# One change to a diffusion backbone kernel on one core: the entry of the first feed forward

## The chip, the core and the metric

The kernel runs on one core of a Trainium2 chip. The core has five engines with their own instruction queues: TensorE (PE, matrix products; PEld is its loading of weights), VectorE (DVE), ScalarE (ACT), GpSimd (POOL) and SyncE (SP, which here only issues transfers), and 16 DMA engines. The metric is device microseconds of one launch. Before the change: 2480.34 us, median of three runs (2479.79 to 2483.69).

## What is computed

Two layers over 640 tokens of width 1024 (512 latent tokens and 128 context tokens), in float32. Each layer is a half-step feed forward, a mixer (pooling, convolution and attention side by side), and a second half-step feed forward. Every one of the three is entered by a normalization and a modulation that depends on a condition vector. Cut to what matters here:

```
def _rms(x, g):
    y = xf * lax.rsqrt(jnp.mean(xf * xf, axis=-1, keepdims=True) + EPS)
    return (y * g.astype(jnp.float32)).astype(x.dtype)

def _modulations(cond, w, b):
    m = jax.nn.silu(cond) @ w + b
    return jnp.split(m[:, None, :], N_MOD, axis=-1)

    sh1, sc1, g1, sh2, sc2, g2, sh3, sc3, g3 = _modulations(cond, p['mod_w'], p['mod_b'])
    h = _rms(x, p['norm_g'][0]) * (1.0 + sc1) + sh1
    x = x + 0.5 * g1 * _swiglu(h, p['ffn1_wi'], p['ffn1_wo'])
    h = _rms(x, p['norm_g'][1]) * (1.0 + sc2) + sh2
    ...
```

For the first feed forward the shift sh1 and the scale sc1 (2048 columns of mod_w of layer 0, 8 MB) are needed before its first matrix product can start, and so is the mean of squares of each token.

## The kernel before

X lies transposed: partitions are features, in 8 chunks (k) of 128, and the free dimension is tokens, cut in two halves of 320. x arrives as five tiles of 128 tokens by 1024 (xt, L199 to L208), is transposed by PE into PSUM and copied to X by DVE.

Matrix products are in fp32 split in a high and a low part (wh, wl for weights; F_h, F_l for the input), three products for one. The feed forward's input has seven forms per pair of chunks (kp = 0 to 3, called quarters here), kept in four tiles F_h and four tiles F_l per layer step; later weight blocks use all seven, the first two blocks (f0 and f1, "plain", L596) only the plain ones.

The entry of the first feed forward (L1204 to L1235) goes like this. The squares of all eight chunks of X are taken by ACT and added by POOL (sq_chunk, L399), PE sums over partitions with a product with ones (r_ss), DVE computes the reciprocal root by three Newton steps (rsqrt), builds a diagonal matrix of it, and PE spreads it over all partitions (r_b), once for each half (rstd_half, L438). ACT copies it to R (L1211). Then, for each of four quarters t, two blocks of modulation weights are loaded (mw, 1 MB each: v = 1 is the scale, v = 0 the shift), PE multiplies them with the condition (mod, L282), DVE transposes the result, adds the bias (modv) and forms the scale a (scale_of). With these, first() and second() make the two halves' plain forms: DVE multiplies X by R (hf_x, hf_q), ACT applies scale and shift (affine, L465; POOL some pieces, L463), ACT and DVE split (F_h L457, F_l L458; hf_A21h and hf_A21l for the second half's even chunk). PE runs that quarter of block f0's four products (plain_step), and sums() makes the other four forms (hf_g). After the fourth quarter come the products of block f1, then the ordinary blocks from 2 on (L555).

Raw weights go through two buffers (tag raw, 8 KB per partition). Quarters 0 and 2 of the modulation weights take these buffers, quarters 1 and 3 take the buffers of F_h and F_l that are not written yet. Transfers are issued by SP in its program order. A scheduler with a timeline of its own decides the order of instructions on every engine from the order of the code and from priorities; so a change at the start can also move instructions far behind it.

Of the kernel before, what the change touches and what calls it, by code (L numbers as in the profile page):

```python
# [98 lines left out]
def backbone(ctx: ExitStack, tc: tile.TileContext, ins, consts, y_prompt, y_sample, out_k, out_v):  # L99
# [96 lines left out]
        par.update(qkg=qkg, sink=sink, nsink=nsink)  # L196


    for i in range(5):  # L199
        xt = act([P, D], F32, f"xt{i}")  # L200
        src = ins["x_sample"][0, i * P:(i + 1) * P, :] if i < 4 else ins["x_prompt"][0]
        nc.sync.dma_start(out=xt, in_=src)
        for q in range(2):
# [65 lines left out]

        return [lambda t=t: step(t) for t in range(4)]  # L270

    def modulation_block(ps, l, v, t, aside):

        if aside:
            raw = scope["pool"].tile([P, KD, 256], F32, tag=f"F{'hl'[v]}", name=f"mw_{l}_{v}_{t}", bufs=4)
        else:
            raw = wpool.tile([P, KD, 256], F32, tag="raw", name=f"mw_{l}_{v}_{t}", bufs=BUFS["raw"])
        nc.sync.dma_start(out=raw, in_=ins["mod_w"][l, :, v * D + 256 * t:v * D + 256 * (t + 1)].rearrange("(k p) f -> p k f", p=P))
        for k in range(KD):
            w = raw[:, k, :].rearrange("p (j g c) -> p j g c", g=4, c=32)  # L280
            for g in range(4):
# [34 lines left out]
            y = y2  # L316
        return y

    def rstd_diag(acc, n, name):

        ps = bank(name + "_ss")
        for i in range(5):
            PE.matmul(ps[:, i:i + 1], acc[:, i * P:(i + 1) * P], ones[:, 0:1], start=True, stop=True)
        v = small(name + "_v", 5)
        V.tensor_scalar(out=v, in0=ps[:, 0:5], scalar1=1.0 / n, scalar2=EPS, op0=ALU.mult, op1=ALU.add)
        y = rsqrt(v, 5, name)
        dg = tmp(name + "_dg")
# [108 lines left out]
    def rstd_half(acc, more, h, name):  # L438

# [774 lines left out]
    pm = [bank(f"mod_0_{v}", "ox"[v]) for v in range(2)]
    chains = [(0, c, h, "asat"[2 * c + h]) for c in range(2) for h in range(2)]
    for t in range(4):
        for v in (1, 0):
            modulation_block(pm[v], 0, v, t, t % 2 == 1)
        scale_of(0, 0, inp.a, slice(2 * t, 2 * t + 2))
        inp.first(R[:, 0:HALF], t)  # L1220
        inp.second(R[:, HALF:T], t)
# [97 lines left out]
```

## Time and profile before

| | |
|---|---|
| median of three runs | 2480.34 us |
| the profiled execution | 2478.26 us, of which 2476.5 us from first to last instruction |
| PE busy / PEld / DVE / ACT / POOL | 2348.3 / 2222.1 / 1707.3 / 1021.5 / 475.7 us |
| the chain that ended last, by engine | PE 82%, DVE 10%, ACT 4%, DMA 2% |
| mean granted clock of TensorE | 0.967 of 2.4 GHz |

Busy time of an engine says where it is full, not whether that matters. PE is the engine of nearly all of the chain, so time is lost where PE waits: in the first 85 us, in the two mixers (about 538 to 831 and 1746 to 2043 us) and a little at the start of the other feed forwards. Idle time of the other engines costs nothing by itself.

### The profile page before, as it was taken

To read this page: it belongs to the slowest core of one execution; us is meant where nothing else is said; L and a number is where in the kernel's file an instruction comes from. 1 tells how busy PE (TensorE), PEld (TensorE's weight loads), DVE (VectorE), ACT (ScalarE), POOL (GpSimd) and SP (SyncE) were. 2 spreads that over 40 slices of the span, in tenths; PEclk is the share of its full clock that TensorE was granted. 3 is DMA by queue.
4 is the path that set the end of the run, shared out by engine and by line. 5 is a ranking of instruction groups with operands and counts; after the bars stand their busy time and mean duration, and the time that the engine had idled before them with its cause. 6 is when DMAs were issued, how large, how long until landed. Compare 5 with 4: busy or idle time off the path is not lost.

```text
span 2476.5 us, 40450 instructions
## 1 busy us (share of the span) xinstructions
PE 2348.3 (95%) x16491; PEld 2222.1 (90%) x16491; DVE 1707.3 (69%) x3174; ACT 1021.5 (41%) x1865; POOL 475.7 (19%) x376
## 2 busy tenths in 40 slices
PE   4999999999888899999989999999988889999999
PEld 4899999998568899999989999999975789999998
DVE  4667676667875876676669484858588569585855
ACT  2433333344674533333345242425266545242423
POOL 2101020121431211111132020212024323020210
PEclk7999999999998999999999999999998899999999
DMA  5444332222512123342312424223243022222222
GB/s 172 131 141 132 98 125 69 92 94 91 181 63 71 49 94 128 104 133 94 121 61 82 141 82 141 86 86 101 73 148 134 22 77 69 86 82 81 86 77 77
DMA packets 193990, 246.04 MB, mean 99 GB/s; under 512 B 5705, under 2 KB 176494, under 8 KB 193804
## 3 DMA queue, kind: packets, MB, share of 16 engines
q1 hardware_dynamic: 191824, 240.81, 29.9%
q8 instruction: 130, 2.13, 0.4%
q0 software_dynamic: 512, 1.95, 0.3%
q10 hardware_dynamic: 1468, 0.70, 0.1%
q14 instruction: 56, 0.46, 0.1%
HBM read 240.55 MB, written 2.88 MB: 98 GB/s over the span
## 4 chain that ended last, share of the span: by engine, by line
PE 82%; DVE 10%; ACT 4%; DMA 2%; issue 2%; SPq 0%; POOL 0%; ACTq 0%; DVEq 0%; POOLq 0%
PE f_B L555 11%; PE o_a L379 11%; PE f_C L555 11%; PE o_b L379 11%; PE f_A L555 11%; PE f_D L555 6%; PE f L596 3%; PE p L743 2%; PE mod L266 2%; PE o L743 1%; PE u_q_b L379 1%; PE u_q_a L379 1%; DVE cy L930 1%; DVE xa_l L397 1%; DVE X L421 1%
## 5 line engine op out<-in xcount | busy, mean ns | idle before, releaser
L379 PE MATMUL o_a<-f_h,o_wh 128*128 128x320 f32 x1344 | 402.9, 310 | 0.0
L379 PE MATMUL o_b<-f_h,o_wh 128*128 128x320 f32 x1344 | 401.4, 309 | 0.0
L421 DVE SCALAR_TENSOR_TENSOR X<-o_a,gate,X 128x320 f32<-128x320 f32 x120 | 65.8, 549 | 305.3 <-PE o_a L379 305.0
L379 PEld LDWEIGHTS o_a<-f_h,o_wh 128*128 128x128 f32 x1344 | 251.0, 188 | 8.7 <-ACT o_wh L358 5.8
L547 POOL TENSOR_TENSOR f_t<-f 128x512 f32<-128x512 f32 x80 | 127.6, 1595 | 660.1 <-DMA f<-in_ffn_wi_dram 556.0
L379 PEld LDWEIGHTS o_b<-f_h,o_wh 128*128 128x128 f32 x1344 | 251.4, 188 | 2.9 <-issue 2.9
L358 ACT ACTIVATE o_wh<-wo 128x768 fp32r<-128x768 f32 (+1 forms) x120 | 95.9, 800 | 381.0 <-PE o_b L379 259.7
L654 POOL TENSOR_TENSOR f_t<-f_t,f 128x512 f32<-128x512 f32 x80 | 114.4, 1430 | 638.1 <-DVE f_q_wl L533 332.8
L379 PE MATMUL o_b<-f_h,o_wl 128*128 128x320 f32 x672 | 207.3, 308 | 0.0
L379 PE MATMUL o_a<-f_h,o_wl 128*128 128x320 f32 x672 | 207.0, 308 | 0.0
L531 ACT ACTIVATE f_q_wh<-f_t 128x512 fp32r<-128x512 f32 x140 | 85.9, 629 | 199.5 <-DVE f_t L545 55.0
L379 PEld LDWEIGHTS o_b<-f_h,o_wl 128*128 128x128 f32 x672 | 126.2, 188 | 0.0
L379 PEld LDWEIGHTS o_a<-f_h,o_wl 128*128 128x128 f32 x672 | 126.0, 188 | 0.0
L359 DVE TENSOR_TENSOR o_wl<-wo,o_wh 128x768 fp32r<-128x768 f32 (+1 forms) x120 | 108.2, 903 | 15.6 <-ACT o_wh L358 15.0
L934 POOL TENSOR_TENSOR cy<-cy,cm 128x655 f32<-128x655 f32 x52 | 88.7, 1705 | 148.4 <-ACT cm L933 148.4
L531 ACT ACTIVATE f_P_wh<-f 128x512 fp32r<-128x512 f32 x112 | 66.5, 626 | 120.2 <-PE f_A L555 78.2
L555 PE MATMUL f_B<-F_h,f_q_wl 128*128 128x320 f32 x352 | 108.7, 309 | 0.8 <-DVE f_q_wl L533 0.8
L555 PE MATMUL f_B<-F_h,f_q_wh 128*128 128x320 f32 x352 | 108.7, 309 | 0.2 <-ACT f_q_wh L531 0.2
L555 PE MATMUL f_B<-F_l,f_q_wh 128*128 128x320 f32 x352 | 108.6, 308 | 0.0
L555 PE MATMUL f_C<-F_h,f_m_wh 128*128 128x320 f32 x336 | 103.6, 308 | 0.0
L555 PE MATMUL f_C<-F_l,f_m_wh 128*128 128x320 f32 x336 | 103.6, 308 | 0.0
L555 PE MATMUL f_C<-F_h,f_m_wl 128*128 128x320 f32 x336 | 103.5, 308 | 0.0
(541 smaller groups left out, 7349.9 us busy)
## 6 DMA issues: line engine op xcount, KB each, us to landing
f<-in_ffn_wi_dram SPq DMA_DIRECT2D x88, 1024.0 KB, 5.2
mw<-in_mod_w_dram SPq DMA_DIRECT2D x72, 1024.0 KB, 5.1
wo<-in_ffn_wo_dram SPq DMA_DIRECT2D x48, 768.0 KB, 4.9
wo<-in_ffn_wo_dram SPq DMA_DIRECT2D x16, 512.0 KB, 3.4
wout<-in_w_out_dram SPq DMA_DIRECT2D x32, 256.0 KB, 3.2
win_q<-in_w_in_dram SPq DMA_DIRECT2D x4, 1024.0 KB, 5.1
xt<-in_x_sample_dram SPq DMA_DIRECT2D x4, 512.0 KB, 5.5
win_cg<-in_w_in_dram SPq DMA_DIRECT2D x2, 1024.0 KB, 5.1
```

The lines of the kernel that those rows point to most:

```text
L266: PE.matmul(ps[32 * g:32 * g + 32, 0:256], C[:, k, :], w[:, :, g, :], start=(k == 0), stop=(k == KD - 1))
L358: A.activation(out=wh, in_=src, func=AF.Copy)
L359: V.tensor_tensor(out=wl, in0=src, in1=wh.bitcast(F32), op=ALU.subtract)
L379: PE.matmul(ps[:, :n], ww[:, k, :], xx[:, lo:lo + n], start=(k == order[0] and i == 0), stop=(k == order[-1] and i == 2))
L421: V.scalar_tensor_tensor(out=X[:, m, s:e], in0=ps[:, s - o:e - o], scalar=gate[:, m, c:c + 1], in1=X[:, m, s:e], op0=ALU.mult, op1=ALU.add)
L531: A.activation(out=h, in_=src, func=AF.Copy, scale=sign)
L547: G.tensor_tensor(out=t3, in0=self.block(g, 1, 1), in1=self.block(g, 0, 1), op=ALU.add)
L555: PE.matmul(ps[:, :HALF], w[:, kp, :], self.F[f][kp][:, i, :], start=(first and kp == 0 and n == 0), stop=(kp == 3 and n == 2), skip_group ...
L596: PE.matmul(ps[:, :HALF], w[:, k, :], x, start=(k == 0 and n == 0), stop=(k == KD - 1 and n == 2))
L654: G.tensor_tensor(out=t2, in0=t2, in1=self.block(g, 1, 0), op=ALU.add)
L743: PE.matmul(ps[:, :HALF], w[:, m % 2, k, :], x[:, h * HALF:(h + 1) * HALF], start=(k == 0 and n == 0), stop=(k == 3 and n == 2))
L934: G.tensor_tensor(out=y, in0=y, in1=m, op=ALU.add)
```

## The change

Four things are done otherwise, all in the entry of the first feed forward.

1. The mean of squares: ACT squares each token tile xt as it arrives (1024 features along the free dimension) and sums along it, which gives one number per token with tokens on partitions. The eight squarings of X, POOL's additions and PE's sums over partitions go. The root is taken once for all five token tiles, and R is spread by rstd_spread, as in the mixers.
2. All eight modulation blocks of shift and scale are loaded at once, each into the buffer of F_h or F_l that the same quarter's form will use later (Input.open opens it after the block has been read).
3. The loads of blocks f0 and f1 are issued between them: f0 behind quarter 0, f1 behind quarter 2.
4. In the code a quarter's modulation products now stand ahead of the previous quarter's products.

```
+    ss00 = small("ss00", 5)
     for i in range(5):
         xt = act([P, D], F32, f"xt{i}")
...
         nc.sync.dma_start(out=xt, in_=src)
+        sq = wpool.tile([P, D], F32, tag="wl", name=f"sqx{i}", bufs=BUFS["w"])
+        A.activation(out=sq, in_=xt, func=AF.Square, accum_out=ss00[:, i:i + 1])
...
-    def modulation_block(ps, l, v, t, aside):
-
-        if aside:
-            raw = scope["pool"].tile([P, KD, 256], F32, tag=f"F{'hl'[v]}", name=f"mw_{l}_{v}_{t}", bufs=4)
-        else:
-            raw = wpool.tile([P, KD, 256], F32, tag="raw", name=f"mw_{l}_{v}_{t}", bufs=BUFS["raw"])
-        nc.sync.dma_start(out=raw, in_=ins["mod_w"][l, :, v * D + 256 * t:v * D + 256 * (t + 1)].rearrange("(k p) f -> p k f", p=P))
+    def modulation_block(ps, l, v, t, raw):
+
...
-    def rstd_diag(acc, n, name):
-
-        ps = bank(name + "_ss")
-        for i in range(5):
-            PE.matmul(ps[:, i:i + 1], acc[:, i * P:(i + 1) * P], ones[:, 0:1], start=True, stop=True)
+    def rstd_diag(acc, n, name, ss=None):
+
+        if ss is None:
+            ss = bank(name + "_ss")
+            for i in range(5):
+                PE.matmul(ss[:, i:i + 1], acc[:, i * P:(i + 1) * P], ones[:, 0:1], start=True, stop=True)
...
+        def __init__(self, l, j, kps=range(4)):
+            self.F, self.nm = ([], []), f"hf{l}{j}"
+            for kp in kps:
+                self.open(kp)
...
+        def open(self, kp):
+            for F, t in zip(self.F, "hl"):
+                F.append(new_form(f"F{self.nm}_{t}{kp}", t).rearrange("p (i t) -> p i t", i=7))
...
     phase("ffn00")
-    acc = tmp("acc00")
-    for k in range(KD):
-        sq_chunk(acc, k, f"sq00_{k}")
-    pbs = [rstd_half(acc, None, h, f"r00{h}") for h in range(2)]
-    R = work.tile([P, T], F32, tag="R", name="R00", bufs=1)
-    for h in range(2):
-        A.activation(out=R[:, h * HALF:(h + 1) * HALF], in_=pbs[h][:, :HALF], func=AF.Copy)
-    inp = Input(0, 0)
+    pm = [bank(f"mod_0_{v}", "ox"[v]) for v in range(2)]
+    inp = Input(0, 0, ())
     f = Ffn(0, 0, inp, ins["ffn1_wi"][0])
-    pm = [bank(f"mod_0_{v}", "ox"[v]) for v in range(2)]
-    chains = [(0, c, h, "asat"[2 * c + h]) for c in range(2) for h in range(2)]
+    raws = {}
     for t in range(4):
         for v in (1, 0):
-            modulation_block(pm[v], 0, v, t, t % 2 == 1)
+
+            raws[t, v] = new_form(f"mw_0_{v}_{t}", "hl"[v], F32)[:, 0:KD * 256].rearrange("p (k f) -> p k f", k=KD)
+            nc.sync.dma_start(out=raws[t, v], in_=ins["mod_w"][0, :, v * D + 256 * t:v * D + 256 * (t + 1)].rearrange("(k p) f -> p k f", p=P))
+        if t % 2 == 0:
+            f.load(t // 2)
+    R = rstd_spread(rstd_diag(None, float(D), "r00", ss00), work.tile([P, T], F32, tag="R", name="R00", bufs=1), [bank(f"r00_{t}", t) for t in "as"])
+    chains = [(0, c, h, "asat"[2 * c + h]) for c in range(2) for h in range(2)]
+
+    def modulations(t):
+        for v in (1, 0):
+            modulation_block(pm[v], 0, v, t, raws[t, v])
+
+    modulations(0)
+    for t in range(4):
+        inp.open(t)
         scale_of(0, 0, inp.a, slice(2 * t, 2 * t + 2))
         inp.first(R[:, 0:HALF], t)
         inp.second(R[:, HALF:T], t)
+        if t < 3:
+            modulations(t + 1)
```

What it does to the order of instructions shows at three places. The first is SP's queue behind x. In mw_0_1_2 the numbers are layer, v and quarter; f00_0 is block f0. Before:

```order
L278 DMA mw_0_1_0_267<-in_mod_w_dram 128x8x256
L278 DMA mw_0_0_0_304<-in_mod_w_dram 128x8x256
L346 DMA f00_0_364<-in_ffn1_wi_dram 128x8x256
L278 DMA mw_0_1_2_535<-in_mod_w_dram 128x8x256
L278 DMA mw_0_0_2_572<-in_mod_w_dram 128x8x256
L278 DMA mw_0_0_1_446<-in_mod_w_dram 128x8x256
L278 DMA mw_0_1_1_409<-in_mod_w_dram 128x8x256
L346 DMA f00_1_793<-in_ffn1_wi_dram 128x8x256
L346 DMA f00_2_915<-in_ffn1_wi_dram 128x8x256
L278 DMA mw_0_0_3_698<-in_mod_w_dram 128x8x256
L278 DMA mw_0_1_3_661<-in_mod_w_dram 128x8x256
L346 DMA f00_3_917<-in_ffn1_wi_dram 128x8x256
```

And of the changed kernel:

```order
L1218 DMA mw_0_1_0_188<-in_mod_w_dram 128x8x256
L1218 DMA mw_0_0_0_190<-in_mod_w_dram 128x8x256
L345 DMA f00_0_192<-in_ffn1_wi_dram 128x8x256
L1218 DMA mw_0_1_1_194<-in_mod_w_dram 128x8x256
L1218 DMA mw_0_0_1_196<-in_mod_w_dram 128x8x256
L1218 DMA mw_0_1_2_198<-in_mod_w_dram 128x8x256
L1218 DMA mw_0_0_2_200<-in_mod_w_dram 128x8x256
L345 DMA f00_1_202<-in_ffn1_wi_dram 128x8x256
L1218 DMA mw_0_1_3_204<-in_mod_w_dram 128x8x256
L1218 DMA mw_0_0_3_206<-in_mod_w_dram 128x8x256
L345 DMA f00_2_872<-in_ffn1_wi_dram 128x8x256
L345 DMA f00_3_874<-in_ffn1_wi_dram 128x8x256
```

The quarters now stand in their order, quarter 3 moved ahead of block f00_2, and the third instruction no longer needs a buffer that quarter 0 used.

The second place is DVE at the start of quarter 0, from the first product of X with R on (hf00_x0; the last digit of hf00_x and hf00_q is the quarter). Before:

```order
L476 TENSOR_TENSOR hf00_x0_342<-X_67,R00_253 128x640
L476 TENSOR_TENSOR hf00_q0_354<-X_67,R00_253 128x640
L476 TENSOR_TENSOR hf00_x1_484<-X_67,R00_253 128x640
L476 TENSOR_TENSOR hf00_q1_494<-X_67,R00_253 128x640
L476 TENSOR_TENSOR hf00_x2_610<-X_67,R00_253 128x640
L476 TENSOR_TENSOR hf00_x3_736<-X_67,R00_253 128x640
L284 STREAM_TRANSPOSE modT_0_1_0_301<-mod_0_1_266 128x64
L284 STREAM_TRANSPOSE modT_0_0_0_338<-mod_0_0_265 128x64
L359 TENSOR_TENSOR f00_0_0_wl_367<-f00_0_364,f00_0_0_wh_366 128x1024
L286 TENSOR_TENSOR modv0_169<-modT_0_1_0_301,mod_b0_88 128x4
L286 TENSOR_TENSOR modv0_169<-modT_0_0_0_338,mod_b0_88 128x4
L359 TENSOR_TENSOR f00_0_1_wl_371<-f00_0_364,f00_0_1_wh_370 128x1024
```

And of the changed kernel:

```order
L481 TENSOR_TENSOR hf00_x0_309<-X_67,R00_229 128x640
L358 TENSOR_TENSOR f00_0_0_wl_402<-f00_0_192,f00_0_0_wh_401 128x1024
L282 STREAM_TRANSPOSE modT_0_0_0_303<-mod_0_0_185 128x64
L358 TENSOR_TENSOR f00_0_1_wl_406<-f00_0_192,f00_0_1_wh_405 128x1024
L481 TENSOR_TENSOR hf00_q0_321<-X_67,R00_229 128x640
L481 TENSOR_TENSOR hf00_x1_447<-X_67,R00_229 128x640
L481 TENSOR_TENSOR hf00_q1_457<-X_67,R00_229 128x640
L284 TENSOR_TENSOR modv0_180<-modT_0_0_0_303,mod_b0_88 128x4
L481 TENSOR_TENSOR hf00_x2_571<-X_67,R00_229 128x640
L481 TENSOR_TENSOR hf00_x3_695<-X_67,R00_229 128x640
L282 STREAM_TRANSPOSE modT_0_1_1_363<-mod_0_1_186 128x64
L284 TENSOR_TENSOR modv0_180<-modT_0_1_1_363,mod_b0_88 128x4
```

Both splits of block f0's weights moved ahead of the second half's product (hf00_q0), and the shift of quarter 0 (modv0 from modT_0_0_0) stands behind three more products of X with R; the scale's part (modT_0_1_0) has gone ahead of all of this. On ACT the order there is R00's first half, the two passes of f00_0_0_wh and f00_0_1_wh, then R00's second half; before, both halves of R00 stood ahead of the two passes.

The third place is ACT in layer 0's attention (a0_2: third pair of heads; cm: multiplications for the convolution's taps), where no line of code was changed. Before:

```order
L933 ACTIVATE cm014_6347<-glu01_5906,taps_1041 128x655
L1099 ACTIVATE a0_2_0S00_6886<-a0_2_0t00_6914 128x384
L826 ACTIVATE mixa01_6353<-a0_1_2o_6768 128x384
L1091 ACTIVATE a0_2_2S20_7006,a0_2_2ls_7001<-a0_2_2S20_7006,a0_2_2nm_7000,rqp02_6318 128x512
L1091 ACTIVATE a0_2_2S21_7011,a0_2_2ls_7001<-a0_2_2S21_7011,a0_2_2nm_7000,rqp02_6318 128x512
L1091 ACTIVATE a0_2_2S30_7016,a0_2_2ls_7001<-a0_2_2S30_7016,a0_2_2nm_7000,rqp02_6318 128x384
L1089 ACTIVATE a0_2_2es_7002<-a0_2_2es_7002 128x6
L1091 ACTIVATE a0_2_2S31_7021,a0_2_2ls_7001<-a0_2_2S31_7021,a0_2_2nm_7000,rqp02_6318 128x384
L1099 ACTIVATE a0_2_0S01_6891<-a0_2_0t01_6920 128x384
```

And of the changed kernel:

```order
L938 ACTIVATE cm015_6307<-glu01_5863,taps_998 128x655
L1104 ACTIVATE a0_2_0S00_6843<-a0_2_0t00_6871 128x384
L831 ACTIVATE mixa01_6310<-a0_1_2o_6725 128x384
L1096 ACTIVATE a0_2_2S20_6963,a0_2_2ls_6958<-a0_2_2S20_6963,a0_2_2nm_6957,rqp02_6275 128x512
L1096 ACTIVATE a0_2_2S21_6968,a0_2_2ls_6958<-a0_2_2S21_6968,a0_2_2nm_6957,rqp02_6275 128x512
L1104 ACTIVATE a0_2_0S01_6848<-a0_2_0t01_6877 128x384
L1096 ACTIVATE a0_2_2S30_6973,a0_2_2ls_6958<-a0_2_2S30_6973,a0_2_2nm_6957,rqp02_6275 128x384
L1096 ACTIVATE a0_2_2S31_6978,a0_2_2ls_6958<-a0_2_2S31_6978,a0_2_2nm_6957,rqp02_6275 128x384
L1096 ACTIVATE a0_2_2S40_6983,a0_2_2ls_6958<-a0_2_2S40_6983,a0_2_2nm_6957,rqp02_6275 128x128
```

The convolution is one tap further at the same point of the attention (cm015 in place of cm014), and a0_2_0S01 has moved ahead of two exponentials. DVE, POOL and PE are interleaved otherwise in the same stage; behind it, up to the end, a few neighbours have changed places.

## Rows read from the trace of the kernel before

**Rows 1.** Stretches: us from:to and length, engines' busy us (instructions), clock, DMA.

```profile
core 0: us, PE busy (x) PEld busy (x) DVE busy (x) ACT busy (x) POOL busy (x), PEclk, DMA share, GB/s
10.00:18.00 8.00, 5.11 (x25) 4.43 (x25) 4.80 (x9) 1.46 (x3) 0.01 (x1) 1.00 1.05 365
18.00:36.00 18.00, 5.88 (x70) 4.70 (x74) 4.50 (x26) 3.96 (x7) 10.70 (x7) 0.50 0.01 2
...
54.00:83.00 29.00, 19.68 (x429) 15.41 (x417) 18.05 (x42) 13.78 (x27) 4.78 (x7) 1.00 0.52 165
83.00:100.00 17.00, 17.00 (x104) 16.82 (x105) 9.18 (x16) 6.78 (x12) 3.65 (x4) 0.90 0.23 69
100.00:520.00 420.00, 419.04 (x2950) 409.20 (x2949) 287.18 (x478) 154.73 (x264) 64.14 (x44) 1.00 0.34 111
```

**Rows 2.** Chain of waits, 0 to 130 us: start us, us, what.

```profile
46.23 10.00 DMA mw<-in_mod_w_dram
...
59.12 6.45 DMA f<-in_ffn_wi_dram
...
82.98 6.49 PE f L596 x32
...
89.82 10.09 PE f L596 x68
```

**Rows 3.** Timeline of the reduction: start us, us, engine, line, operation.

```profile
15.22 1.29 DVE L208 COPY X<-xT 128x512 f32<-128x512 f32 x2 [0.18 <-PE xT L207]
...
17.98 11.19 POOL L405 TENSOR_TENSOR acc<-acc,sq 128x640 f32<-128x640 f32 x7 [13.62 <-ACT sq L404]
...
30.90 0.17 DVE L309 TENSOR_SCALAR r_y<-r_v 128x3 int32<-128x3 int32 x1
...
32.67 0.16 DVE L315 SCALAR_TENSOR_TENSOR r_y<-r_w,r_y 128x3 f32<-128x3 f32 x1
...
34.23 1.44 PE L453 MATMUL r_b<-r_dg,ones 128*128 128x320 f32 x2
...
35.70 0.44 ACT L1211 ACTIVATE R<-r_b 128x320 f32<-128x320 f32 x1 [14.04 <-PE r_b L453]
```

**Rows 4.** One instruction of four lines: count, ns min/median/max, first and last start.

```profile
L1091 ACT ACTIVATION_READ_ACCUMULATOR a_2S<-a_2S,a_2nm,rqp x48: 185/187/190, 615.7 to 1952.4; 128x1 f32 x48
...
L358 ACT ACTIVATE f_wh<-f x3: 1040/1057/1057, 41.6 to 65.6; 128x1024 fp32r<-128x1024 f32 x3
L359 DVE TENSOR_TENSOR f_wl<-f,f_wh x3: 1217/1224/1226, 42.7 to 66.7; 128x1024 fp32r<-128x1024 f32 x3
...
L458 DVE TENSOR_TENSOR F_l<-hf_g,F_h x16: 1476/1491/2273, 52.4 to 2068.0; 128x1280 fp32r<-128x1280 f32 x16
```

**Rows 5.** Tile xt, its transfers from issue to landing.

```profile
DMA to landing us min/median/max: 4.5/6.2/7.7
```

**Rows 6.** Timeline: the last x tile's issue on SP, two waits of PE for blocks.

```profile
6.11 0.33 SPq L202 DMA_DIRECT2D xt<-in_x_prompt_dram  x1
...
53.44 0.94 PEld L282 LDWEIGHTS mod<-mw,C 128*32 128x32 f32 x64 [0.19 <-DMA mw<-in_mod_w_dram]
56.28 0.94 PEld L282 LDWEIGHTS mod<-mw,C 128*32 128x32 f32 x64 [1.89 <-DMA mw<-in_mod_w_dram]
```

**Rows 7.** Timeline of DVE: starts of 640-wide products and of 320-wide differences.

```profile
40.60 1.55 DVE L476 TENSOR_TENSOR hf_x<-X,R 128x640 f32<-128x640 f32 x2
...
49.29 0.48 DVE L501 TENSOR_TENSOR hf_g<-hf_q 128x320 f32<-128x320 f32 x1
49.70 0.48 DVE L503 TENSOR_TENSOR hf_g<-hf_q,hf_p 128x320 f32<-128x320 f32 x1
```

**Rows 8.** Timeline of ACT, fourth quarter: scale and shift, then first F_h.

```profile
78.73 1.20 ACT L465 ACTIVATE hf_p<-hf_x,modv,a 128x320 f32<-128x320 f32 x2 [3.55 <-DVE modv L286]
...
80.65 0.46 ACT L457 ACTIVATE F_h<-hf_p 128x320 fp32r<-128x320 f32 x1
```

**Rows 9.** Stretches from the mixer's R to the next feed forward, layers 0, 1.

```profile
538.30:831.00 292.70, 256.58 (x1778) 215.05 (x1776) 208.89 (x487) 161.92 (x336) 81.65 (x73) 0.93 0.28 93
1746.60:2042.70 296.10, 261.87 (x1776) 218.98 (x1774) 209.33 (x486) 161.96 (x336) 81.78 (x73) 0.91 0.27 92
```

More of the change, by code (lines that the diff above doesn't have):

```diff
@@ L317, in rsqrt @@
         return y
-    def rstd_diag(acc, n, name):
-        ps = bank(name + "_ss")
-        for i in range(5):
-            PE.matmul(ps[:, i:i + 1], acc[:, i * P:(i + 1) * P], ones[:, 0:1], start=True, stop=True)
+    def rstd_diag(acc, n, name, ss=None):
[3 more added lines that the diff above has]
+                PE.matmul(ss[:, i:i + 1], acc[:, i * P:(i + 1) * P], ones[:, 0:1], start=True, stop=True)
         v = small(name + "_v", 5)
-        V.tensor_scalar(out=v, in0=ps[:, 0:5], scalar1=1.0 / n, scalar2=EPS, op0=ALU.mult, op1=ALU.add)
+        V.tensor_scalar(out=v, in0=ss[:, 0:5], scalar1=1.0 / n, scalar2=EPS, op0=ALU.mult, op1=ALU.add)
         y = rsqrt(v, 5, name)
@@ L427, in gate_of, with new_form @@
         return gv
-    def new_forms(name):
-        return [[scope["pool"].tile([P, 7, HALF], F32R, tag=f"F{t}", name=f"{name}_{t}{kp}", bufs=4) for kp in range(4)] for t in "hl"]
+    def new_form(name, t, dt=F32R):
+        return scope["pool"].tile([P, 7 * HALF], dt, tag=f"F{t}", name=name, bufs=4)
     def rstd_half(acc, more, h, name):
@@ L467, in backbone @@
     class Input:
-        def __init__(self, l, j):
-            self.F, self.nm = new_forms(f"F{l}{j}"), f"hf{l}{j}"
+        def __init__(self, l, j, kps=range(4)):
+            self.F, self.nm = ([], []), f"hf{l}{j}"
+            for kp in kps:
+                self.open(kp)
             self.a, self.sh = small(f"a_{l}_{j}", 16).rearrange("p (k c) -> p k c", c=2), modv[l][:, 3 * j]
             self.hp, self.hq = {}, {}
+        def open(self, kp):
+            for F, t in zip(self.F, "hl"):
+                F.append(new_form(f"F{self.nm}_{t}{kp}", t).rearrange("p (i t) -> p i t", i=7))
         def scaled(self, dst, pb, h, kp):
```

## The prediction

> **What bounds the kernel now.** I read three views in this order: the stretches, to see which engine is full where; the chain of waits over the first 130 us, to see what the entry waits for; and the timeline of the entry, for durations. The stretches show two different kernels. From 100 to 520 us PE is busy 419.04 of 420 us at full clock [rows 1]: there only PE's own work counts, and what another engine does earlier or later costs nothing. From 18 to 83 us PE is mostly idle. Between 18 and 36 us the DMA moves 2 GB/s, that is nothing, although weights that are needed next are known by then, and TensorE's granted clock is 0.50, the 1.2 GHz level [rows 1]. The chain of waits then names two long transfers, 10.00 us for modulation weights and 6.45 us for feed-forward weights [rows 2]. The entry therefore works as a series: a reduction without transfers, then transfers that wait for buffers. Dense PE work starts with the first product of the fourth quarter's low part (F_l) at 82.98 us; 32 + 68 = 100 products of the first two weight blocks are left then [rows 2]. So the change is worth what it takes from that 82.98, plus what happens to work further on that is moved by accident.
>
> **The sum of squares.** Removed are eight squarings of X on ACT, seven additions on POOL that take 11.19 us from 17.98 on, twelve tiny PE products and one of two rsqrt chains; R's first half reaches ACT at 35.70 [rows 3]. Added are five squarings of token rows with a running sum on ACT. The trace of before has no square with a sum, so I bound it: a 1024-wide ACT pass takes 1.06 us, and reading a sum adds 0.19 us (187 ns) [rows 4], 1.25 us together; if the sum doubled the pass it would be 2.3. The last x tile is issued at 6.11 us and lands within 4.5 to 7.7 us [rows 5, 6], so by 13.8; with 1.25 us the sums stand near 14.5 to 15, with 2.3 near 16.5. DVE's copies of X end at 15.22 + 1.29 = 16.5 in either case [rows 3] and stand ahead of the chain, so I take 1.25 and the difference is hidden by these copies. Then come v (0.2) and ten steps of rsqrt; in before the ten start between 30.90 and 32.67 [rows 3], 0.197 us apart, so 2.0; two small steps of the first modulation stand among them (0.4), and the 640-wide diagonal costs about 0.8 (two 640-wide products in 1.55 us [rows 7]). That gives 19.9 us. The spread over PE takes 1.44 and the copy 0.44 [rows 3]: R's first half is there near 21.9 instead of 36.1, 14 us earlier.
>
> **The loads.** SP now issues all eight modulation blocks and the first two feed-forward blocks behind x, without a wait for a buffer. The DMA moves 365 GB/s while it is full and falls still at 18 us, when x and the first two blocks are in [rows 1]. A block of 1.05 MB then takes 2.9 us, and eight more follow without a gap: first feed-forward weights at 21, quarter 1 at 24 and 27, quarter 2 at 30 and 33, second feed-forward weights at 36, quarter 3 at 38 and 41 us. In before the blocks of quarter 1 landed at 53.4 and 56.2 [rows 6]. What is queued behind on SP is the third feed-forward block; it waits for DVE to have split the first one, near 25 us, and its turn comes at 41, so it isn't held. POOL's and ACT's queues issue nothing in this stretch that they did not issue before.
>
> That blocks land one by one is read off two waits of PE for modulation blocks, 53.44 and 56.28, 2.84 us apart [rows 6], which is one block's time. The Trainium skill's page "DMA: Bandwidth & Descriptors", section "Queues, rings and completion order", says that completion isn't first in, first out per issuing engine. By the rows the sum is as above; by the rule early blocks could land with the late ones, which is the second rival below.
>
> **The four quarters.** With the data in place DVE and ACT set the pace. ACT copies R's first half, then stands behind the first feed-forward block (21) for two passes of 1.06 [rows 4], and only then copies R's second half, near 24.5; DVE splits the same weights (2 x 1.22 [rows 4]) to 25.3 and does three 640-wide products (0.78 each [rows 7]) before it finishes the shift of quarter 0, at 27.7. From there ACT needs 1.92 us to its first F_h (78.73 to 80.65 [rows 8]): 29.7. Up to the scale of quarter 3, DVE has 46 instructions: four of 640 (3.1), 24 of 320 at 0.41 (49.29 to 49.70 [rows 7], 9.8), two of 1280 (1.49 [rows 4], 3.0), one of 1.22 and 15 small ones at 0.2 (3.0), together 20.1 us. Following the new order row by row with ACT's durations I get 22.3, so DVE idles about 2 us and that scale is ready at 50.0. ACT finishes a 1280-wide pass at 51.0, adds 1.92, and DVE's first low part of quarter 3 follows at 54.2, where before had 82.98: **28.8 us earlier**. In the new order 97 products are left at that point, not 100, worth 3 x 0.15 (68 in 10.09 us [rows 2]) or 0.4.
>
> Each cost at nothing has its cover. The buffers of F that hold modulation weights are read out by PE near 45 for quarter 3 and first written near 51, so 6 us of cover. PE has 41 products between the second quarter's start near 46 and 54: 6.0 us at 0.147, cover 2 us.
>
> **The clock.** Between 18 and 36 us, with PE busy 5.88 us, the granted clock is 0.50; between 54 and 83, busy 19.68 of 29 with gaps, it is 1.00; between 83 and 100, after waits for F_h and F_l, it is 0.90 [rows 1]. In the new order PE is busy in about the share of the 54 to 83 stretch from 30 us on, so I take 1.00, with a fall like that of 83 to 100 once. The bound the other way: 41 products at the 1.2 GHz level take twice as long, 12 us in place of 6.0, which would pass the 54.2 by about 4 us; and a clock that doesn't fall at all would give back the 10% of 17 us, 1.7. The Trainium skill's "TensorE: Matmul & The Clock Gate", Part 1, says that an idle array goes back to half rate and stays there until activity has been sustained. By the row the sum is 28.8; by the rule, if the gaps before quarters 2 and 3 count as idle, it is about 25.
>
> **What moves by accident.** The order behind the first feed-forward block is unchanged up to the attention stage of layer 0; there ACT, DVE, POOL and PE are interleaved otherwise. The trace shows two orders of the same stage: 292.7 us in layer 0, with 256.6 of PE, and 296.1 us in layer 1, where the two orders differ about as much [rows 9]. So another order is worth some 3.4 us; as layer 0 has the better of the two, I add half, 1.7, and keep -4 to +8.
>
> **Sum.** The profiled execution took 2478.26 us. 2478.26 - 28.8 - 0.4 + 1.7 = 2450.8. The median of the runs is 2480.34, 2.1 higher, so for a median I say **2453 us**.
>
> **Rivals.**
> *The PE stage gives part back.* The attention stage of layer 0 loses 8 to 20 us in its new order: 2461 to 2473. For it: 36 us of that stage are without PE work and its clock is 0.93 [rows 9], so there is room to lose. Against it: two very different orders are 3.4 apart.
> *Blocks land together.* If the eight share the rate, quarter 0 starts at about 41 us in place of 27.7 and the quarters follow DVE's 22.3 and 4.2 us later: 68 in place of 54.2, a gain of 15, 2466. Against it stand the two waits of rows 6.
> *The loads are not what holds.* If the quarters had been bound by DVE and ACT in before too, only the 14 us of the reduction would come: 2480.3 - 14 = 2466. Against it: ACT waits 10.00 and 6.45 us for transfers in the chain [rows 2].
> *Slower.* One mechanism could do it: the attention stage of layer 0, if DVE's or ACT's moved steps keep PE waiting long enough to let the clock fall. Its time without PE work would have to grow from 36.1 us by more than 28.8, to over 65; if it doubled, the time would be 2453 - 1.7 + 36 = 2487. Nothing in the rows of its two orders points there.
>
> **How the numbers follow.** Forecast as above, 2441 to 2461: 0.78. Attention gives part back, 2461 to 2473: 0.10. Blocks together or loads not the limit, about 2466: 0.07. A loss in the attention stage that leaves less than 5 us of gain or makes it slower: 0.05, of which 0.03 slower. The range 2441 to 2466 takes in the clock (+4, -1.7), the attention stage (-4, +8) and most of the two cases at 2466. About 0.2%, 5 us, is what a measurement of this kernel can tell from no change; faster than that 0.94, within it 0.03, slower 0.03.
>
> **What would show it.** Right: DMA full from 10 to about 42 us without the hole at 18; the square with sum near 1.25 us; R's first copy near 21.5; F_h first at 29 to 31, and the fourth quarter's F_l product at 53 to 56; the same 17 us behind it; layer 0's attention within 289 to 301. Wrong: modulation products that wait for transfers beyond 30 us, a granted clock of 0.5 past 40 us, or an attention stage over 301 us.

## The result and the profile after

The changed kernel takes 2454.41 us (median of four runs, 2454.11 to 2454.92); the kernel before took 2480.07 beside it (four runs, 2476.77 to 2483.69). The ratio is 0.9903, with a 95% interval of 0.9891 to 0.9914. The profiled execution took 2454.21 us, with a span of 2452.4.

The stretches of the kernel after, in the columns of rows 1. The DMA hole from 18 to 36 us [rows 1] is gone: transfers run at 349 to 370 GB/s through 30 us and beyond. PE is full from 57 us on (16.83 of 17 us) as it was from 83 on, and at clock 1.00 where before had 0.90.

```profile
10.00:18.00 8.00, 4.46 (x89) 3.70 (x89) 6.96 (x23) 3.34 (x6) 0.00 (x0) 0.97 1.07 370
18.00:30.00 12.00, 7.30 (x165) 5.45 (x169) 7.09 (x12) 3.86 (x6) 1.02 (x1) 0.50 1.10 349
30.00:54.00 24.00, 21.32 (x381) 19.59 (x371) 20.60 (x49) 16.22 (x32) 7.20 (x9) 0.83 0.70 221
57.00:74.00 17.00, 16.83 (x110) 16.20 (x111) 9.58 (x16) 7.79 (x14) 3.65 (x4) 1.00 0.21 69
75.00:500.00 425.00, 422.31 (x2963) 411.79 (x2962) 290.96 (x481) 155.46 (x264) 66.76 (x45) 1.00 0.34 112
```

The timeline of the kernel after, ACT: one square with its sum (last of five), R's first half, the first passes over block f0. A square takes 1.06, its sum 0.19, and the copy of R's first half starts at 21.43 in place of 35.70 [rows 3]. The passes over f0 wait for a transfer until 23.0.

```profile
12.88 1.06 ACT L205 ACTIVATE sqx<-xt 128x1024 f32<-128x1024 f32 x1 [0.18 <-DMA xt<-in_x_prompt_dram]
13.84 0.19 ACT L205 ACTIVATION_READ_ACCUMULATOR sqx<-xt 128x1 f32 x1
21.43 0.44 ACT L335 ACTIVATE R<-r_a 128x320 f32<-128x320 f32 x1 [7.41 <-PE r_a L334]
23.01 2.00 ACT L357 ACTIVATE f_wh<-f 128x1024 fp32r<-128x1024 f32 x2 [1.14 <-DMA f<-in_ffn_wi_dram]
```

PE's waits for quarter 0's blocks end at 15.94 and 18.95, ACT's wait for the first feed-forward block at 23.0: as far as waits show it the blocks land one by one, and early blocks that land with the late ones, the prediction's second rival, don't show here. From 18.95 to 23.0 the DMA moved 350 GB/s, which is 1.4 MB in 4.05 us and more than the one block of 1.05 MB, so a part of it was for blocks behind.

```profile
15.94 1.10 PE L280 MATMUL mod<-mw,C 128*32 128x64 f32 x64 [2.01 <-DMA mw<-in_mod_w_dram]
18.95 1.08 PE L280 MATMUL mod<-mw,C 128*32 128x64 f32 x32 [1.91 <-DMA mw<-in_mod_w_dram]
```

```profile
18.95:23.00 4.05, 4.05 (x60) 2.62 (x64) 0.82 (x1) 0.44 (x1) 0.00 (x0) 0.50 1.09 350
```

SP's queue in the kernel after: from the third block on the issue of one block takes SP about as long as a block needs to move (3.74; 12.98 for four). The last line is the third feed-forward block, issued at 35.2, and with it the DMA is full until 45.

```profile
6.63 1.77 SPq L1218 DMA_DIRECT2D mw<-in_mod_w_dram  x2
9.12 3.74 SPq L345 DMA_DIRECT2D f<-in_ffn_wi_dram  x1
12.90 12.98 SPq L1218 DMA_DIRECT2D mw<-in_mod_w_dram  x4
25.92 2.83 SPq L345 DMA_DIRECT2D f<-in_ffn_wi_dram  x1
28.80 6.30 SPq L1218 DMA_DIRECT2D mw<-in_mod_w_dram  x2
35.21 2.82 SPq L345 DMA_DIRECT2D f<-in_ffn_wi_dram  x1
```

The timeline of the kernel after round quarter 3: DVE's scale of it, POOL's two pieces and its sum for weight block 2, DVE beside them, PE's first F_l product. POOL's pieces take 3.00 us and hf_g, which is 0.48 elsewhere [rows 7], takes 1.58 beside POOL's sum.

```profile
50.41 0.15 DVE L301 SCALAR_TENSOR_TENSOR a<-modv,vec 128x4 f32<-128x4 f32 x1
50.73 3.00 POOL L462 TENSOR_SCALAR hf_q<-hf_q,a,modv 128x192 f32<-128x192 f32 x2 [5.64 <-issue]
52.01 1.48 DVE L457 TENSOR_TENSOR Fhf_l<-hf_g,Fhf_h 128x1280 fp32r<-128x1280 f32 x1
53.70 1.29 POOL L552 TENSOR_TENSOR f_t<-f 128x512 f32<-128x512 f32 x1
53.77 1.58 DVE L506 TENSOR_TENSOR hf_g<-hf_q 128x320 f32<-128x320 f32 x1 [0.28 <-POOL hf_q L462]
57.01 0.42 PE L601 MATMUL f<-Fhf_l,f_wh 128*128 128x320 f32 x1 [0.87 <-DVE Fhf_l L457]
```

The chain of waits after has the same stretch of 68 products that before had at 89.82 [rows 2], now 27.30 us earlier:

```profile
62.52 10.08 PE f L601 x68
```

Where the gain stands further on is read by putting the same product of both traces side by side and subtracting their starts. This table has that difference (us earlier than the profiled execution of before) near five times of before, for every kernel run, and in the last column the difference of the medians, each against the kernel before on the same chip.

| kernel | 300 | 545 | 905 | 1700 | 2440 | median |
|---|---|---|---|---|---|---|
| after | 27.30 | 27.30 | 23.26 | 23.34 | 24.04 | -25.7 |
| e1 squares only | 14.76 | 14.79 | 14.36 | 14.47 | 17.13 | -16.1 |
| e2 loads only | 12.86 | 14.45 | 19.20 | 19.13 | 21.38 | -15.5 |
| e3 f1 last | 27.85 | 29.44 | 29.41 | 29.47 | 32.09 | -29.7 |
| e4 quarter 3 on ACT | 25.57 | 28.68 | 25.36 | 25.52 | 26.21 | -25.1 |
| e5 other order | 27.24 | 27.27 | 27.26 | 28.53 | 35.52 | -34.1 |
| e6 no POOL | 27.74 | 27.78 | 25.40 | 25.47 | 27.88 | -27.7 |
| e7 f0 behind quarter 1 | 22.24 | 25.38 | 23.39 | 23.45 | 26.45 | -26.0 |
| e8 e3 with e5 | 28.21 | 29.81 | 30.23 | 30.33 | 33.76 | -33.8 |
| e9 pieces on DVE | 26.78 | 26.80 | 26.80 | 26.82 | 29.12 | -27.7 |

In the kernel after the entry brings 27.30 us, nothing changes up to 545, 4.0 are given back between 545 and 905 (layer 0's mixer and the entry of the feed forward behind it), and 0.7 come back in layer 1. The stretches of rows 9, by the same end points in the kernel after: 295.10 in place of 292.70, and 295.40 in place of 296.10.

```profile
511.00:806.10 295.10, 257.70 (x1778) 217.19 (x1776) 210.34 (x487) 162.71 (x336) 80.40 (x73) 0.93 0.27 92
1723.00:2018.40 295.40, 258.39 (x1778) 216.06 (x1776) 209.46 (x487) 162.13 (x336) 80.99 (x73) 0.92 0.27 92
```

### The profile page after: what moved, and what is told of

The parts are those of the page before. It is cut to its first block, busy times and chain, and to the rows that moved or that the text cites. A ratio compares the mean times of both kernels' runs of the same rounds, so it can differ in the third digit from the quotient of the medians.

```text
span 2452.4 us, 40409 instructions
## 1 busy us (share of the span) xinstructions
PE 2340.1 (95%) x16479; PEld 2218.7 (90%) x16479; DVE 1706.3 (70%) x3160; ACT 1023.1 (42%) x1867; POOL 462.5 (19%) x369
## 4 chain that ended last, share of the span: by engine, by line
PE 82%; DVE 11%; ACT 4%; issue 2%; DMA 1%; POOL 0%; SPq 0%; ACTq 0%; DVEq 0%
PE f_B L560 11%; PE o_a L378 11%; PE f_C L560 11%; PE f_A L560 11%; PE o_b L378 11%; PE f_D L560 6%; PE f L601 3%; PE p L748 2%; PE mod L269 2%; DVE cy L935 1%; PE u_q_b L378 1%; PE u_q_a L378 1%; DVE xa_l L396 1%; PE o L748 1%; ACT a_2S L1096 1%
## 5 line engine op out<-in xcount | busy, mean ns | idle before, releaser
L560 PE MATMUL f_B<-Fhf_h,f_q_wl 128*128 128x320 f32 x352 | 108.4, 308 | 0.8 <-DVE f_q_wl L538 0.8
L560 PE MATMUL f_B<-Fhf_h,f_q_wh 128*128 128x320 f32 x352 | 108.4, 308 | 0.2 <-ACT f_q_wh L536 0.2
L560 PE MATMUL f_B<-Fhf_l,f_q_wh 128*128 128x320 f32 x352 | 108.2, 308 | 0.0
L560 PE MATMUL f_C<-Fhf_h,f_m_wh 128*128 128x320 f32 x336 | 103.3, 308 | 0.0
L560 PE MATMUL f_C<-Fhf_l,f_m_wh 128*128 128x320 f32 x336 | 103.3, 308 | 0.0
L560 PE MATMUL f_C<-Fhf_h,f_m_wl 128*128 128x320 f32 x336 | 103.2, 308 | 0.0
```

Of the source, the lines that this page charges most:

```text
L560: PE.matmul(ps[:, :HALF], w[:, kp, :], self.F[f][kp][:, i, :], start=(first and kp == 0 and n == 0), stop=(kp == 3 and n == 2), skip_group ...
```

## The experiments

**e1 and e2: each part alone.** e1 puts the new squares, root and R into the kernel before; e2 puts the old ones into the kernel after.

```diff
 e1, from before:                                   (e2, from after: the reverse)
-    acc = tmp("acc00")
-    for k in range(KD):
-        sq_chunk(acc, k, f"sq00_{k}")
-    pbs = [rstd_half(acc, None, h, f"r00{h}") for h in range(2)]
...
+    R = rstd_spread(rstd_diag(None, float(D), "r00", ss00), ...)
```

> The kernel before, with the squares, the root and R of the kernel after; loads, their buffers and the order of the quarters stay as before. Behind the entry the order of instructions is that of the kernel before, the mixer included. Theory A (reduction and loads stood in series, each held the entry for a part): R's first half is ready near 21.5 us in place of 36, PE reads quarter 0's blocks near 20, the first feed-forward block is issued there and not at 36.5, and the rest of the chain follows as before, 14 to 16 us earlier: first F_l product of quarter 3 at 67 to 69, time 2464 to 2467. The mixer of layer 0 takes as long as before (anchor to anchor 317.6 us). Rival (the loads were hidden anyway, DVE and ACT set the pace): the whole gain of the entry comes from here, time 2450 to 2455.

> The kernel after, with the squares, POOL's sums and the two root chains of the kernel before; the loads at once stay. Theory A: R comes at 36, all quarters' weights are there or land by 45, so the quarters follow at the pace of DVE and ACT: first F_l product of quarter 3 at 68 to 71, 12 to 15 us earlier than before (82.98); time 2465 to 2468, and since the mixer's order is a third one, up to 4 us to either side. Rival (loads hidden anyway): no gain, 2476 to 2484. If the two parts alone gain 14 and 13, they add up to the 27.3 of both.

e1: 2461.09 us (2458.13 to 2462.00), ratio 0.9929 (0.9916 to 0.9941). The chain of waits of e1 still has the series of transfers; only its start moved, since f0's load is issued at 17.40 and not at 36.52. The first F_l product of quarter 3 comes at 67.76, within the 67 to 69 that were expected.

```profile
17.40 7.84 DMA f<-in_ffn_wi_dram
...
29.91 10.71 DMA mw<-in_mod_w_dram
...
43.31 6.34 DMA f<-in_ffn_wi_dram
```

e2: 2461.66 us (2456.86 to 2463.23), ratio 0.9928 (0.9916 to 0.9941). R comes at 35.84, the first F_l product of quarter 3 at 71.42, a little behind the 68 to 71 that were expected, and PE waits for no block between quarters; POOL's pieces of quarter 3 again take 3.01.

```profile
35.84 0.44 ACT L1224 ACTIVATE R<-r_b 128x320 f32<-128x320 f32 x1 [11.91 <-PE r_b L449]
71.42 0.42 PE L598 MATMUL f<-Fhf_l,f_wh 128*128 128x320 f32 x1 [0.93 <-DVE Fhf_l L454]
```

At 300 us the parts gain 14.76 and 12.86, together 27.62; both at once gain 27.30. So reduction and loads stood one behind the other, each part is worth about half, and neither hid the other: theory A holds, the rival falls. e1's time lies 3 us below what was expected, and its trace gains 2.7 in layer 1's mixer; e2 gains 4.75 more in layer 0's mixer, which has a third order there. But e2's trace is of the fastest of its five executions (2456.86, median 2461.66), so at its end the table shows 21.38 where the medians have 15.5.

**e3: who takes back the 4 us.** The second feed-forward block is loaded behind quarter 3. In layer 0's mixer every engine then has the order of the kernel before.

```diff
-        if t % 2 == 0:
-            f.load(t // 2)
+        if t == 0:
+            f.load(0)
+        if t == 3:
+            f.load(1)
```

> The kernel after, with the load of the second feed-forward block issued behind quarter 3 in place of quarter 2. That moves some DVE and ACT steps of quarters 2 and 3 and brings, by the scheduler, the order of the kernel before back in the mixer of layer 0. Theory B (the 4 us given back between 613 and 856 us come from the mixer's new order and nothing else): the entry gains 27 +- 1, and the gain stays that size to the end: time 2450 to 2451.5, the stage from 538 to 856 takes 317.6 as before. Rival (it is given back by the clock or by transfers that come earlier, whatever the order): 2454 to 2455, stage 321 to 322.

2447.54 us (2446.13 to 2447.84), ratio 0.9876 (0.9861 to 0.9891): 2.5 us below the 2450 to 2451.5 that were expected, and its trace gains 1.6 between 300 and 545 (a step of the clock, shown in the last section) and another 2.6 in layer 1's mixer. From 545 to 905 it gives back 0.03, where the kernel after gives back 4.04. e1, with before's order too, gives back 0.43; e4, with the order of the kernel after and another entry, 3.32. From the first product that spreads the mixer's R to the first f_A of the next feed forward, the kernel after, e4, e3 and e2, in this sequence:

```profile
511.04:819.39 308.35, 270.76 (x1854) 229.74 (x1852) 223.26 (x507) 171.28 (x352) 86.11 (x78) 0.93 0.26 88
```

```profile
509.66:817.32 307.66, 270.56 (x1854) 228.71 (x1852) 223.18 (x507) 170.91 (x352) 86.45 (x78) 0.93 0.26 88
```

```profile
508.90:814.91 306.01, 269.46 (x1854) 227.46 (x1852) 222.03 (x507) 170.55 (x352) 87.26 (x78) 0.93 0.26 89
```

```profile
523.89:825.12 301.23, 265.91 (x1854) 225.09 (x1852) 221.69 (x507) 170.42 (x352) 86.53 (x78) 0.95 0.26 90
```

In these traces the give-back follows the order, not the entry, as theory B has it. Of the 2.3 us between the kernel after and e3 in these rows, 1.3 are PE's busy time and 1.0 is waiting; the rest up to 4 lies just behind the first f_A. How sure this is: in layer 1's mixer all engines have the same order in the kernel after, e3, e4 and e9, and yet the kernel after and e4 gain 0.7 there, e3 2.6 and e9 2.3. So one and the same order varies by 2 us. The 4.0 and 3.3 are above that; the 2.0 and 2.4 of e7 and e6 are not, or hardly. Whole executions of one kernel, in which the order is the same by construction, lie further apart: e4's four from 2445.37 to 2454.03, e2's five from 2456.86 to 2463.23, and a trace is of one of them. The four of the kernel after (2454.11 to 2454.92) and of e3 lie close together; their medians, each against the kernel before on its chip, differ by 4.0, with intervals that meet at 0.9891, while the two traces end 8.05 apart. That the 4.0 of the mixer are the order's is likely by this, not settled.

**e4, e6, e9: POOL beside DVE.** e4 gives quarter 3's odd pieces to ACT, e9 those of all quarters to DVE, e6 also the third sum of weight block 2.

```diff
 e4:   if h and k % 2 and own != "ACT":          (own is "ACT" in quarter 3 of the entry)
 e9:   (V if own == "DVE" else G).tensor_scalar(...)      (all four quarters of the entry)
 e6:   as e9, and
-            G.tensor_tensor(out=t3, ...)
+            (V if (self.l, self.j, g) == (0, 0, 2) else G).tensor_tensor(out=t3, ...)
```

> The kernel after, with the second half's odd chunk of quarter 3 scaled and shifted by ACT (0.85 us) in place of POOL (3.00 us there); behind the entry no instruction is ordered otherwise. Theory C (POOL and DVE hold each other up where both read SBUF: POOL's two pieces take 3.00 in place of 0.93, DVE's hf_g 1.58 in place of 0.48): ACT's first F_h of quarter 3 comes 0.6 later (54.4), DVE's steps behind take 0.48 again, the first F_l product comes at 55.3 to 56.0 in place of 57.01, and the time is 1.0 to 1.7 less, 2452.7 to 2453.4. Rival (ACT's own queue or PE holds quarter 3): the time stays or grows by the 0.6 to 0.9 that ACT has more, 2454.4 to 2455.3.

> The kernel after with POOL taken out of the quarters: the odd chunks' pieces of all four quarters and the third sum of weight block 2 are done by DVE. Theory C (POOL and DVE hold each other up where both read SBUF): without POOL no DVE operation of the entry is stretched, the 320-wide ones with two inputs all take 0.48 (after: up to 1.58; e4: up to 1.42); from the scale of quarter 3 to the first F_l product it is 5 to 5.7 us in place of 6.6, though DVE has eight pieces and one sum more (estimate 2.5 to 3.5 us over the entry); the first F_l product comes at 55.5 to 58. Rival (the stretch has another cause, ACT or transfers): some 320-wide DVE operations of the entry still take over 0.9 us.

> The kernel after with the odd chunks' pieces of the four quarters done by DVE; POOL keeps only the third sum of weight block 2, which meets DVE's work near 54 as in the kernel after. In the mixer of layer 0 the order is nearer to e2's (301.2 us) than that of e5 (305.9) is. Theory C: one DVE operation of 320 or 512 columns is stretched to 1.2 to 1.7 us beside POOL's sum, none else; entry gain 27 to 28. Theory B: the layer 0 mixer takes 301 to 305; time 2446 to 2451. Rival: 306 to 309 and 2453 to 2455.

e4: 2452.14 us (2445.37 to 2454.03), ratio 0.9889 (0.9875 to 0.9904): no difference from the kernel after that the intervals tell. In the entry it is 1.7 slower, not 1.0 to 1.7 faster. Its timeline, POOL, DVE, ACT and PE: POOL, free earlier, took the sum for block 2 at 47.45, beside other work of DVE, and the stretch moved there; ACT's four pieces came on top. The first F_l product comes at 56.90, 0.11 earlier than in the kernel after and not at 55.3 to 56.0: ahead of it PE waits 2.05 us for ACT's F_h, and from 56.2 to 59.0 the granted clock is 0.50, where the kernel after has 1.00 behind 57.0. So ACT's own queue holds quarter 3 here, as the rival has it, and the 1.7 us were lost behind the F_l product, where the low clock is one cause.

```profile
47.21 0.82 DVE L481 TENSOR_TENSOR hf_q<-X,R 128x640 f32<-128x640 f32 x1
47.45 1.73 POOL L552 TENSOR_TENSOR f_t<-f 128x512 f32<-128x512 f32 x1 [2.02 <-DMA f<-in_ffn_wi_dram]
48.11 1.42 DVE L457 TENSOR_TENSOR Fhf_l<-hf_p,Fhf_h 128x320 fp32r<-128x320 f32 x1
54.05 1.74 ACT L464 ACTIVATE hf_q<-hf_q,modv,a 128x192 f32<-128x192 f32 x4
56.20 0.90 PE L601 MATMUL f<-Fhf_h,f_wh 128*128 128x320 f32 x2 [2.05 <-ACT Fhf_h L456]
```

These rows show how the two engines hold each other up. POOL's sum is issued while DVE's product runs (to 48.03) and ends 1.15 behind it, at 49.18; DVE's 320-wide step is issued at 48.11 and ends 0.35 behind POOL, at 49.53. In the kernel after it is the same: POOL's sum ends at 54.99, DVE's hf_g 0.36 later. So each runs alone, in the order in which they came (POOL's sum takes 1.29 by itself, DVE's step 0.48). The Trainium skill's page "SBUF — State Buffer", section "Who interferes with whom", says so: a VectorE instruction with two SBUF inputs and a GpSimd instruction that reads SBUF exclude each other, and the one that comes second waits for the whole of the first. By this rule the trace agrees.

e6: 2451.59 us (2450.34 to 2453.95), ratio 0.9893 (0.9875 to 0.9910). With POOL idle, all 320-wide steps of DVE in the entry take 0.45 to 0.49, and from the scale of quarter 3 (50.41) to the first F_l product (56.13) it is 5.72 us in place of 6.60, though DVE does a pair of pieces in 0.64 and the sum in 0.69 itself. The timeline of DVE in e6:

```profile
50.61 0.64 DVE L462 TENSOR_SCALAR hf_q<-hf_q,a,modv 128x192 f32<-128x192 f32 x2
53.78 0.69 DVE L552 TENSOR_TENSOR f_t<-f 128x512 f32<-128x512 f32 x1
54.38 0.48 DVE L506 TENSOR_TENSOR hf_g<-hf_q 128x320 f32<-128x320 f32 x1
```

e9: 2450.26 us (2445.46 to 2451.54), ratio 0.9885 (0.9870 to 0.9899). Exactly one step is stretched, 1.42 at 48.38 beside POOL's sum (47.74, 1.70); the entry gains 26.78, a little under what was expected, and the mixer took 305.93, not 301 to 305, which is nearer to the rival's 306 to 309, though the time is within the 2446 to 2451 that were expected. Nearness to e2's order foretold nothing. Theory C holds for the durations. For the end it is worth little: 0.44 us of entry in e6, since DVE has POOL's work to do instead.

**e5 and e8: other orders.** One number of the scheduler's priorities in the mixer.

```diff
 e5, from after; e8, from e3:
-AHEAD = 200
+AHEAD = 190
```

> The kernel after with one constant of the scheduler's priorities in the mixer changed (AHEAD 190 in place of 200). Up to layer 0's mixer every engine has the instructions of the kernel after in the same order; in the mixer the order is another one, of the five measured so far nearest to that of e2, which took 301.2 us from the first spread product (r_x) to the first f_A behind, against 308.4 in the kernel after and 306.0 in the kernel before. Theory B (the order of that stage decides what it takes): entry gain 27.3 +- 0.6 at 500 us, the stage 300 to 305, a gain over the kernel before of 28 to 34 us. Rival (the stage varies by itself, with the clock, whatever the order): 306 to 309, gain 23 to 27.

> e3 (second feed-forward block loaded behind quarter 3) with the constant of e5 (AHEAD 190). Layer 0's mixer has nearly e3's order, layer 1's a somewhat other one than e3's, but not that of e5. Theory B: entry gain 27.8 at 200 us and nothing given back in layer 0's mixer (27.3 to 29.5 at 905), then in layer 1 between 1 and 8 us more, so that the gain over the kernel before ends at 29 to 36, time at 2444 to 2450. Rival (the order does not decide): 24 given, 2454 to 2456.

e5: 2445.19 us (2442.71 to 2446.45), ratio 0.9865 (0.9848 to 0.9883). The entry is that of the kernel after (27.24), nothing is given back in layer 0's mixer (its stage 305.93, between the 300 to 305 that were expected and the rival's 306 to 309, so the stage doesn't decide), and layer 1's gains 7.0. What decides is the time: 34.1 us by the medians, where the rival had 23 to 27, with an interval clear of that of the kernel after. One constant of the order moves the time by 8 us. e5's trace is of its fastest execution (2442.71). Layer 1's stage in the kernel after and in e5:

```profile
1723.03:2032.65 309.62, 272.48 (x1854) 229.75 (x1853) 223.37 (x509) 171.43 (x353) 86.70 (x78) 0.92 0.26 88
```

```profile
1714.78:2020.73 305.95, 269.52 (x1853) 228.25 (x1852) 224.92 (x508) 171.19 (x353) 86.39 (x78) 0.93 0.26 89
```

e8: 2444.19 us (2443.81 to 2444.95), ratio 0.9864 (0.9847 to 0.9880): within the 2444 to 2450 expected, and with e5 the best kernel here. Both beat the kernel after, whose interval begins at 0.9891. Against e3, whose interval is 0.9861 to 0.9891, e8's 4 us by the medians are within the noise.

**e7: f0 later.** The first feed-forward block is loaded behind quarter 1, the second behind quarter 3.

```diff
-        if t % 2 == 0:
-            f.load(t // 2)
+        if t == 1:
+            f.load(0)
+        if t == 3:
+            f.load(1)
```

> The kernel after with the loads in another order: the first feed-forward block behind quarter 1, the second behind quarter 3. Theory D (in the kernel after, quarter 0 waits for the landing of the first feed-forward block at 23.0, since ACT's and DVE's passes over it stand ahead; but the entry's end is set by DVE's row of work, about 29 us busy of 36): the first F_h comes at 24 to 27 in place of 30.8, the first F_l product of quarter 3 gains less than half of that, 54 to 57 in place of 57.0. Rival (the landing sets the end): the block lands near 29, six us later, and the first F_l product comes at 61 to 63; or, the other way, all six us are gained, 51. The order of the mixer differs, which may move the time by up to 5 us.

2453.27 us (2451.78 to 2455.69), ratio 0.9897 (0.9881 to 0.9913). The entry gains only 22.24: theory D falls. The first F_h comes at 29.33, not 24 to 27, and the first F_l product of quarter 3 at 60.09, three us late and not early (the rival had 61 to 63). The other two us of the loss come behind it, where the granted clock is 0.50 from 60 to 66. The timeline of e7, ACT and DVE round the second block, and DVE's scale of quarter 2:

```profile
44.54 1.06 ACT L357 ACTIVATE f_wh<-f 128x1024 fp32r<-128x1024 f32 x1 [2.35 <-DMA f<-in_ffn_wi_dram]
45.63 1.23 DVE L358 TENSOR_TENSOR f_wl<-f,f_wh 128x1024 fp32r<-128x1024 f32 x1 [1.03 <-ACT f_wh L357]
46.78 0.16 DVE L301 SCALAR_TENSOR_TENSOR a<-modv,vec 128x4 f32<-128x4 f32 x1
```

The pass over the late block stands on ACT and DVE ahead of the scale of quarter 2, which comes at 46.78 in place of 43.72. In e3 the block is loaded at the same time (both issue it near 32), but its passes stand behind that scale, which comes at 41.39, and the entry gains 0.55 against the kernel after. A landing counts by what is queued behind the step that waits for it. POOL and DVE also met once more, POOL's two pieces of quarter 1 taking 4.21 us at 30.82.

## Why the prediction was right in the time and where it was not

The mechanism was right: two waits stood one behind the other, and taking both away brought nearly the sum that was worked out. That the time, 2454.41 for 2453 predicted, agrees better than the steps is luck: two terms were mis-sized the same way, and the margin between profile and median went the other way.

- **The reduction**: right in its end, 1.25 us for a square with its sum and R's first half there at 21.87 for 21.9, but by two errors that cancel. DVE's copies of X end at 15.20, not 16.5, and its chain with the diagonal at 18.29, not 19.9. Then R's product on PE stands behind quarter 0's products, which wait for a block until 18.95, and starts at 19.96; that wait I had not listed.
- **The loads**: right in kind, one by one and without a gap, and mis-sized: f0 lands at 23.0 and not 21. The lower rate, 349 GB/s in place of 365, makes little of that; the second block of quarter 0 landed at 18.95 and not by 18, and then f0 took 4.05 us and not 2.9, while the DMA also moved parts of later blocks. The DMA is full to 45, not 42: the rate makes about 1 us, and the third feed-forward block, which follows at once, is not in the 42. f0's landing costs the first quarter 1 us: its first F_h comes at 30.84, predicted 29.7.
- **The pace of DVE and ACT**: right. From the shift of quarter 0 (28.71, predicted 27.7) it is 21.7 us for 22.3, and the scale of quarter 3 stands at 50.41, predicted 50.0; e1 and e2 show that both parts were needed for it.
- **From there to the first F_l product**: wrong, 57.01 for 54.2. The working took POOL's pieces as free and every DVE step at the duration it has alone. POOL's pieces took 3.00 and hf_g 1.58, and the order put both ahead of F_l: 6.60 us from the scale to that product, where the working has 4.2. e6 and e9 show that the stretch comes and goes with POOL. Its price on the end is less than the 2.8 us: 0.9 in e6 at that product, since DVE has POOL's 0.64 and 0.69 to do there (5.72 less these two is 4.4, an estimate of what it would be without either). The trace of before showed the stretch at the same place, with 1.67 for POOL's pieces and 1.27 for hf_g:

```profile
78.85 1.67 POOL L463 TENSOR_SCALAR hf_q<-hf_q,a,modv 128x192 f32<-128x192 f32 x2 [13.27 <-issue]
80.49 1.27 POOL L547 TENSOR_TENSOR f_t<-f 128x512 f32<-128x512 f32 x1
80.85 1.27 DVE L501 TENSOR_TENSOR hf_g<-hf_q 128x320 f32<-128x320 f32 x1 [0.65 <-ACT hf_q L465]
```

- **The clock**: a stretch of 0.90 behind the entry was expected, and it was 1.00. With the three products fewer (0.4) that gave 1.3 back: 25.97 at the first F_l product, 27.30 at the 68 products behind it. From 30 to 54 us it was 0.83, not the 1.00 I took, and from 48.2 to 51.5, behind a hole of 1.94 us in PE's work, 0.50, which I had named as a sign of being wrong. DVE set the pace there: PE still waits 0.87 us for F_l at 57.01, so that product didn't depend on it.
- **The entry together**: 27.30 for 28.8 + 0.4.
- **The reordered mixer**: 4.04 given back for 1.7, within the -4 to +8. The sign was a guess from two orders; e1, e3 and e4 speak for the order as its cause, with the limits named at e3. The stage itself, 295.10, lies within the 289 to 301 that I had given.
- **Sum**: 1.9 less in the entry, 2.3 more in layer 0, 0.7 back in layer 1: the profiled execution should have taken 2450.8 and took 2454.21. The median lies only 0.2 above it, where 2.1 were added for that.
- **A loose reading**: PE is not "mostly idle" from 18 to 83 us. From 54 to 83 it is busy 19.68 of 29 [rows 1]. The sum doesn't use it.

## What to carry to other kernels

Where an entry waits for a reduction and then for transfers, taking one of them away brings only its own part (here 14.8 and 12.9 of 27.3): look for both. When the order is chosen by a scheduler, compare a change by the same instruction's start at several places and not by the end alone; here one number in the priorities was worth 8 us (e5 against the kernel after, where the whole change brought 25.7). One trace is one execution: look at how far apart the kernel's other executions lie before a few us in it are explained. Before moving a load, look at what stands behind its first reader on that reader's engine.

## What the runs showed of the hardware that I had not expected

GpSimd and VectorE ran one at a time where both read SBUF: up to 1.58 in place of 0.48 for a 320-wide step of VectorE, 1.67 to 4.21 in place of 0.94 for GpSimd's pair.

The granted clock falls or doesn't fall after one and the same wait. At the start of layer 0's mixer PE waits 0.59 and then 1.13 us for xa_l, in the same order in every kernel. The 10 to 12 us behind it, in the kernel after, e3 and e4:

```profile
499.00:511.00 12.00, 12.00 (x65) 12.00 (x64) 4.34 (x17) 1.65 (x2) 0.00 (x0) 0.73 0.27 89
```

```profile
498.00:509.00 11.00, 11.00 (x66) 11.00 (x67) 4.27 (x17) 1.78 (x2) 0.00 (x0) 0.84 0.30 98
```

```profile
500.00:509.70 9.70, 9.42 (x66) 9.42 (x67) 4.50 (x18) 1.72 (x2) 0.08 (x1) 1.00 0.35 111
```

In the table this shows between 480 and 545 us as steps of 0, 1.6 and 3.1 us (the kernel after, e3, e4). Each is one execution of its kernel, and what decides between the three isn't shown; such a step must not be put down to a change.

With several 1 MB blocks outstanding, SP's issue of one takes 2.8 to 4.0 us, about as long as a block moves (3.0 at 349 GB/s). PE had a hole of 1.94 us at 45.4 in the middle of quarter 3's modulation products, with a release by nothing that the profile shows; no run was made for it, and its cause stays open.
